# Landing x once and computing the forget sums with heads on partitions, in a decoder block on one core

## The chip, the cores and the metric

The kernel runs on one core of a Trainium2 chip. Its time is the device time of one execution in microseconds (us). Five engines matter. PE (TensorE) multiplies matrices: a weight load brings a stationary tile into the array, a matmul streams a moving tile through it, and the results go to PSUM, which has eight banks here (128 partitions by 512 fp32 words each). DVE (VectorE), ACT (ScalarE) and POOL (GpSimd) work elementwise, and SP (SyncE) issues DMAs. Each engine runs its own list of instructions in order, and waits on semaphores for what other engines or DMA queues have done.

## The reference: what is computed

One decoder layer on x, 256 tokens by 1024 channels, in fp32. With h = rms_norm(x), one projection gives q, k, v of two attention branches of 8 heads of 64, one forget logit per token and head, and two sets of gate logits. The first branch (moba) is, with 256 tokens and blocks of 256, plain causal softmax attention with a partial rotary embedding. The second one is what this change touches:

```python
log_f = jax.nn.log_sigmoid(f_logit + b_forget)      # (B, S, 8), then heads first
c = jnp.cumsum(log_f, axis=-1)                       # running sum over the tokens
s = einsum('bhcd,bhsd->bhcs', q, k) * HEAD_DIM**-0.5
s = s + c[t] - c[s]                                  # then causal mask and softmax
```

The two branch outputs go through their own output projections, are weighted with sigmoid gates, added, projected and added to x. A gated feed-forward layer with a causal convolution of width 3 follows.

## The kernel before

**Precision.** Each fp32 weight tile and each activation is split in a high part in fp32r and a low part (`whi`, `wlo`, `xh`, `xl`); a product is three matmuls (hi·hi, lo·hi, hi·lo). ACT writes `whi` (L123, a copy), DVE writes `wlo` (L124, raw minus `whi`) for every unit of weights. That is most of both engines' work.

**Loads.** Weights come by SP in the order of a list of units. A raw tile of 128x2048 (three buffers, tag `raw`) holds two units; a unit's split goes into one of six `whi`/`wlo` buffers, five units ahead of its use. The first eight units are the "heads": one DMA (two for heads 0 and 1) brings into one raw buffer, side by side, 256 tokens of the transposed x for 128 channels, the norm gain, and 1024 weight columns of q and k (L105). `split_x` makes `xh` and `xl` from x times gain (L155 to L158), `square_x` squares x on ACT (L162) and POOL adds the squares up (L164, L166). After the heads come the small tables (L192), and then the other weights.

**Stages.** `project_qk` (L233) multiplies the eight heads, `norm1` turns the sums of squares into `rs`, the norm factor of each token with tokens on partitions (L204). `project(m, ...)` (L243) then makes v, and q, k, v of the second branch; between them stand the small steps: `finish_qk` (norms and rotary), `turn_qk` (L291, transposes), the forget steps and the score matmuls of branch 0 (L393) with their softmax on DVE and ACT (L405 to L413; the profile's operation there is a fused add-and-minimum with an accumulator). `turn(0)` transposes the 48 blocks of probabilities into six banks (L423), ACT evicts them, and the gate matmuls (L457 to L459) begin.

**The forget steps.** `forget_a` loads nothing itself: the transposed x, `xT`, has come by two separate DMAs of 512 KB (L495), and eight small matmuls (L309) give the logits of the heads in four row groups of a bank. Two more matmuls (L312) spread `rs` over all partitions with tokens along the row; DVE copies it out as `rsB` (L315), which scales the gate logits later (L466). `forget_b` adds the row groups with two matmuls (L322), which puts tokens on partitions: everything up to the log sigmoid `lf` is 128 partitions by 2x8. `forget_c` makes the cumulative sum `cc` with three matmuls against a triangle and ones (L348 to L350). `forget_d` turns `cc` over (L356), DVE copies it out (L358), and two DMAs on ACT's queue write it to DRAM and read it back onto all partitions (L360, L362). `forget_bias` then makes the bias of the second branch's scores (L369, L371).

**What sets the order.** PE's order is that of the program (`manual_schedule`). The other engines' lists are made by a scheduler that places instructions by priority; what stands in a `with soon():` block comes 45 steps earlier in priority. PSUM tiles rotate through the eight banks, so a bank is written again only when the last reader of its earlier tile is done.

The lines that the change and the steps of the prediction touch:

Of the kernel before, what the change touches and what calls it, by code (L numbers as in the profile page):

```python
# [43 lines left out]
def decoder_block(ctx, tc, a, out):  # L44
# [52 lines left out]
    def load(upto):  # L97
        while state["next"] <= min(upto, len(units) - 1):
            c, h = units[state["next"]]
            if c[0] == "head":  # L100
                k = c[1]
                raw = T([P, 2048], "raw", RB)
                cuts = (0, HX + W4, HEADW) if k < 2 else (0, HEADW)
                for s0, s1 in zip(cuts, cuts[1:]):
                    loads[c] = nc.sync.dma_start(raw[:, s0:s1], a["head"][k][:, s0:s1])  # L105
                x, g, raw = raw[:, 0:S], raw[:, S:S + 1], raw[:, HX:HEADW]
# [32 lines left out]

    sm = T([P, C_END], "sm")  # L140
    g1 = T([P, KT], "g1")

# [47 lines left out]
    def tables():  # L190
        for t, n in ((sm, "smalls"), (cst, "consts"), (wfr, "wf"), (g1, "g1")):
            after(nc.sync.dma_start(t, a[n]), loads["head", KT - 1])  # L192
        nc.vector.tensor_scalar_mul(gq, sm[:, C_QG:C_QG + 4:2], -HD ** -0.5)
        nc.vector.tensor_tensor(wfg[:, :, 0:NH], wfr, g1[:, :, None].to_broadcast([P, KT, NH]), op=ALU.mult)
# [103 lines left out]
    gates = T([P, KT, 2, S], "gates")  # L298
# [6 lines left out]
    def forget_a():  # L305
# [4 lines left out]
        rp = fp[:, S:]  # L310
        for t in range(NT):
            nc.tensor.matmul(rp[:, t * P:(t + 1) * P], rs[:, t:t + 1].to_broadcast([P, P]), ident, start=True, stop=True)  # L312
        fs = gates[:, 0, 0]
        nc.vector.tensor_copy(fs, fp[:, :S])
        nc.vector.tensor_copy(rsB, rp)  # L315
        fg["fs"] = fs

    def forget_b():
        fs = fg["fs"]
        ft = bank()  # L320
        for t in range(NT):
            nc.tensor.matmul(ft[:, t * NH:(t + 1) * NH], fs[:, t * P:(t + 1) * P], sel, start=True, stop=True)  # L322
        z = T([P, NT, NH], "z")
        for t in range(NT):
            nc.vector.scalar_tensor_tensor(z[:, t], ft[:, t * NH:(t + 1) * NH], rs[:, t:t + 1], col(C_BF, NH), op0=ALU.mult, op1=ALU.add)

        az = T([P, NT, NH], "az")
        nc.scalar.activation(az, z, AF.Abs)
        e = T([P, NT, NH], "ez")
        nc.scalar.activation(e, az, AF.Exp, scale=-1.0)  # L330
        u = T([P, NT, NH], "uz")
        nc.vector.tensor_scalar_add(u, e, 1.0)
        l = T([P, NT, NH], "lz")
        nc.scalar.activation(l, u, AF.Ln)
        d = T([P, NT, NH], "dz")
        nc.vector.scalar_tensor_tensor(d, u, -1.0, e, op0=ALU.add, op1=ALU.subtract)
        r = T([P, NT, NH], "rz")
# [3 lines left out]
        lf = T([P, NT, NH], "lf")  # L341
        nc.vector.scalar_tensor_tensor(lf, z, 0.0, l, op0=ALU.min, op1=ALU.subtract)
        fg["lf"] = lf

    def forget_c():
        lf = fg["lf"]
        cp = bank()
        nc.tensor.matmul(cp[:, 0:8], tri, lf[:, 0], start=True, stop=True)  # L348
        nc.tensor.matmul(cp[:, 8:16], ones, lf[:, 0], start=True, stop=False)
        nc.tensor.matmul(cp[:, 8:16], tri, lf[:, 1], start=False, stop=True)  # L350
        nc.vector.tensor_copy(cc, cp[:, 0:16].rearrange("p (t h) -> p t h", t=NT))

    def forget_d():
        ctp = bank()
        for t in range(NT):
            nc.tensor.transpose(ctp[:8, t * P:(t + 1) * P], cc[:, t], ident)  # L356
        cT = gates[:NH, 1, 0]
        nc.vector.tensor_copy(cT, ctp[:8, :S])  # L358
        cd = dr.tile([NH, S], F32, name="cd")
        nc.scalar.dma_start(cd, cT)  # L360
        cB = gates[:, 4:].rearrange("p a b t -> p (a b) t")
        nc.scalar.dma_start(cB, bass.AP(tensor=cd.tensor, offset=cd.offset, ap=[[0, P], [S, NH], [1, S]]))  # L362
        fg["cB"] = cB
# [116 lines left out]
    pq, pk, pv = banks(), banks(), banks()  # L480
    for k in range(KT):
# [3 lines left out]
    with soon():  # L485
        norm1()
        qn, kn = finish_qk(0, ((0, pq), (1, pk)))
# [6 lines left out]
    for j in range(2):  # L494
# [237 lines left out]
```

## Time and profile before

| what | value |
|---|---|
| median of three runs | 365.48 us (365.46 to 365.97) |
| the profiled execution | 365.81 us, its span 364.0 us |
| granted clock | 1.0 |
| PE busy | 359.7 us, 99% of the span |
| DVE busy | 271.4 us, 75% |
| ACT busy | 215.3 us, 59% |
| POOL busy | 17.5 us, 5% |
| HBM read | 67.69 MB, 189 GB/s over the span |

The span runs from the first to the last instruction of the profiled execution; its time is 1.8 us longer, which lies around it. A row of the timeline gives start, length, engine, line, operation, output and input tiles, shapes and a count, and in brackets the idle time of the engine before it with what ended it. The lengths of pipelined instructions overlap, so the time an instruction takes on its engine is read from one start to the next.

### The profile page before, as it was taken

What the parts mean: (1) busy time and instruction counts of PE and PEld (TensorE: products, weight loads), DVE (VectorE), ACT (ScalarE), POOL (GpSimd) and SP (SyncE); (2) the same over time, 40 slices, a digit from 0 to 9 for tenths busy, and PEclk for the clock granted to TensorE, in tenths of its full rate; (3) what the DMA queues carried; (4) which work ended last, traced back from release to release, by engine and by line L of the source; (5) the groups of instructions that cost most, each with busy time, mean ns of one, the idle gap of its engine ahead of it and who ended that gap; (6) DMA issues with size and microseconds to landing.
All of it is one profiled execution on the core that took longest, in us unless ns stands there. A gap on an engine that the chain in (4) does not pass through costs nothing.

```text
span 364.0 us, 7218 instructions
## 1 busy us (share of the span) xinstructions
PE 359.7 (99%) x2975; PEld 340.2 (93%) x2975; DVE 271.4 (75%) x471; ACT 215.3 (59%) x358; POOL 17.5 (5%) x21
## 2 busy tenths in 40 slices
PE   9999999999999999999999999999999999999996
PEld 5888878888999999999999999999999999999995
DVE  4858998981999656984979867777686777768653
ACT  5748686776559885544867645545555545546420
POOL 0540000000000000000430000000000000000000
PEclk9999999999999999999999999999999999999999
DMA  8798875436081663645654554645645654644003
GB/s 281 236 337 314 325 298 196 158 117 233 2 330 25 232 225 115 220 159 204 230 177 170 206 186 188 232 147 202 230 157 194 230 174 176 230 170 180 1 2 115
DMA packets 11425, 69.21 MB, mean 190 GB/s; under 512 B 1528, under 2 KB 1920, under 8 KB 3968
## 3 DMA queue, kind: packets, MB, share of 16 engines
q1 hardware_dynamic: 11232, 67.69, 51.6%
q10 hardware_dynamic: 160, 1.06, 0.8%
q8 instruction: 23, 0.38, 0.4%
q14 instruction: 10, 0.08, 0.1%
HBM read 67.69 MB, written 1.06 MB: 189 GB/s over the span
## 4 chain that ended last, share of the span: by engine, by line
PE 99%; DVE 0%; issue 0%
PE bank L457 15%; PE bank L459 15%; PE bank L458 15%; PE bank L243 12%; PE bank L233 6%; PE bank L647 6%; PE bank L645 5%; PE bank L646 5%; PE bank L549 2%; PE bank L575 2%; PE bank L550 2%; PE bank L576 2%; PE bank L551 2%; PE bank L577 2%; PE bank L393 2%; PE bank L439 2%
## 5 line engine op out<-in xcount | busy, mean ns | idle before, releaser
L124 DVE TENSOR_TENSOR wlo<-raw,whi 128x1024 fp32r<-128x1024 f32 (+1 forms) x124 | 149.3, 1211 | 48.3 <-ACT whi L123 46.7
L123 ACT ACTIVATE whi<-raw 128x1024 fp32r<-128x1024 f32 (+1 forms) x124 | 128.5, 1044 | 85.5 <-PE bank L458 45.8
L457 PE MATMUL bank<-oh,whi 128*128 128x256 f32 x352 | 97.1, 276 | 0.0
L459 PE MATMUL bank<-oh,wlo 128*128 128x256 f32 x352 | 97.0, 275 | 0.0
L458 PE MATMUL bank<-ol,whi 128*128 128x256 f32 x352 | 97.0, 275 | 0.0
L457 PEld LDWEIGHTS bank<-oh,whi 128*128 128x128 f32 x352 | 66.1, 188 | 0.0
L458 PEld LDWEIGHTS bank<-ol,whi 128*128 128x128 f32 x352 | 66.1, 188 | 0.0
L459 PEld LDWEIGHTS bank<-oh,wlo 128*128 128x128 f32 x352 | 66.1, 188 | 0.0
L457 PE MATMUL bank<-xh,whi 128*128 128x256 f32 x128 | 35.8, 279 | 0.0
L459 PE MATMUL bank<-xh,wlo 128*128 128x256 f32 x128 | 35.3, 276 | 0.0
L458 PE MATMUL bank<-xl,whi 128*128 128x256 f32 x128 | 35.3, 276 | 0.0
L457 PEld LDWEIGHTS bank<-xh,whi 128*128 128x128 f32 x128 | 24.0, 188 | 0.5 <-DVE gates L466 0.3
L458 PEld LDWEIGHTS bank<-xl,whi 128*128 128x128 f32 x128 | 24.1, 188 | 0.0
L459 PEld LDWEIGHTS bank<-xh,wlo 128*128 128x128 f32 x128 | 24.0, 188 | 0.0
L243 PE MATMUL bank<-whi,xh 128*128 128x512 f32 x64 | 20.1, 395 | 0.0
L612 DVE TENSOR_TENSOR sq<-bank,rs 128x512 f32<-128x512 f32 x22 | 15.1, 692 | 6.6 <-PE bank L459 6.5
L243 PE MATMUL bank<-whi,xl 128*128 128x512 f32 x64 | 19.7, 389 | 0.0
L243 PE MATMUL bank<-wlo,xh 128*128 128x512 f32 x64 | 19.7, 389 | 0.0
L549 PE MATMUL bank<-oh,whi 128*128 128x256 f32 x64 | 17.8, 277 | 0.0
L550 PE MATMUL bank<-ol,whi 128*128 128x256 f32 x64 | 17.6, 276 | 0.0
L551 PE MATMUL bank<-oh,wlo 128*128 128x256 f32 x64 | 17.6, 276 | 0.0
L645 PE MATMUL bank<-kT,whi 128*128 128x256 f32 x64 | 17.6, 276 | 0.0
(161 smaller groups left out, 730.1 us busy)
## 6 DMA issues: line engine op xcount, KB each, us to landing
raw<-in_wu SPq DMA_DIRECT2D x22, 1024.0 KB, 4.8
raw<-in_wd SPq DMA_DIRECT2D x11, 1024.0 KB, 4.8
raw<-in_qkv SPq DMA_DIRECT2D x8, 1024.0 KB, 6.8
raw<-in_wg SPq DMA_DIRECT2D x8, 1024.0 KB, 4.8
raw<-in_wb SPq DMA_DIRECT2D x4, 1024.0 KB, 4.8
raw<-in_wo SPq DMA_DIRECT2D x4, 1024.0 KB, 4.9
raw<-in_head SPq DMA_DIRECT2D x6, 644.0 KB, 4.9
xT<-in_xT SPq DMA_DIRECT2D x2, 512.0 KB, 6.8
```

The costliest lines, as they stand in the source:

```text
L123: i = nc.scalar.activation(hi[:, s], raw[:, s], AF.Copy)
L124: d = nc.vector.tensor_tensor(lo[:, s], raw[:, s], hi[:, s].bitcast(F32), op=ALU.subtract)
L233: nc.tensor.matmul(pt[t], lhs[:, k, t * P:(t + 1) * P], rhs, start=(k == 0 and i == 0), stop=(k == KT - 1 and i == 2))
L243: nc.tensor.matmul(pt[t], lhs[:, k, t * P:(t + 1) * P], rhs, start=(k == 0 and i == 0), stop=(k == KT - 1 and i == 2))
L457: nc.tensor.matmul(o, wh[:, w], mh[:, k], start=(k == 0 and i == 0), stop=False)
L458: nc.tensor.matmul(o, wh[:, w], ml[:, k], start=False, stop=False)
L459: nc.tensor.matmul(o, wl[:, w], mh[:, k], start=False, stop=(k == KT - 1 and i == 1))
L549: nc.tensor.matmul(o, wh[:, w], oh[:, 4 * br + k], start=(k == 0), stop=False)
L550: nc.tensor.matmul(o, wh[:, w], ol[:, 4 * br + k], start=False, stop=False)
L551: nc.tensor.matmul(o, wl[:, w], oh[:, 4 * br + k], start=False, stop=(k == 3))
L645: nc.tensor.matmul(o, wh[:, w], ah, start=(p == 0 and h == 0 and c == 0), stop=False)
L647: nc.tensor.matmul(o, wl[:, w], ah, start=False, stop=(last and h == 1 and d == ds[-1]))
```

## The change

x lands once. Heads 0 and 1 land in the space of `gates`, which is not used until later, and POOL copies their x into `xT`. For heads 2 to 7 x lands directly in `xT` by a DMA of its own, and the weights take half a raw buffer. The gain `g1` comes first, by a DMA on ACT's queue. The two DMAs of `xT` are gone.

`rsB` comes by DRAM: after `norm1` POOL's queue carries two DMAs of 128 words into `rd` and one that reads it back onto all partitions. L312 and L315 are gone.

The forget sums stand with heads on partitions: one matmul (`sel` stationary, the 256 tokens moving) gives 8 partitions by 256, the log sigmoid is computed in that shape in rows of `gates`, and a scan on DVE along the tokens replaces the triangle matmuls. `cT` goes to DRAM and back by two DMAs on POOL's queue, as soon as the scan is done. `cc` (tokens on partitions) comes from two small transposes of `cT`, where `forget_d` was. The bias of the logits lies as a column on 8 partitions.

```diff
--- before.py
+++ after.py
@@ -99,11 +99,19 @@
             c, h = units[state["next"]]
             if c[0] == "head":
                 k = c[1]
-                raw = T([P, 2048], "raw", RB)
-                cuts = (0, HX + W4, HEADW) if k < 2 else (0, HEADW)
-                for s0, s1 in zip(cuts, cuts[1:]):
-                    loads[c] = nc.sync.dma_start(raw[:, s0:s1], a["head"][k][:, s0:s1])
-                x, g, raw = raw[:, 0:S], raw[:, S:S + 1], raw[:, HX:HEADW]
+                if k < 2:
+                    raw = gates[:, 4 * k:4 * k + 4].rearrange("p a b t -> p (a b t)")
+                    for s0, s1 in ((0, HX + W4), (HX + W4, HEADW)):
+                        loads[c] = nc.sync.dma_start(raw[:, s0:s1], a["head"][k][:, s0:s1])
+                    x, g, raw = raw[:, 0:S], raw[:, S:S + 1], raw[:, HX:HEADW]
+                    nc.gpsimd.tensor_copy(xT[:, k], x)
+                else:
+                    if k % 2 == 0:
+                        state["raw"] = T([P, 2048], "raw", RB)
+                    raw = state["raw"][:, k % 2 * 1024:(k % 2 + 1) * 1024]
+                    x, g = xT[:, k], g1[:, k:k + 1]
+                    nc.sync.dma_start(x, a["head"][k][:, 0:S])
+                    loads[c] = nc.sync.dma_start(raw, a["head"][k][:, HX:HEADW])
                 xlo = split_x(k, x, g)
                 at, n = 44, 2 if k < 2 else 1
             else:
@@ -137,8 +145,10 @@
         return split.pop((c, h))
 
 
+    gates = T([P, KT, 2, S], "gates")
     sm = T([P, C_END], "sm")
     g1 = T([P, KT], "g1")
+    nc.scalar.dma_start(g1, a["g1"])
 
     def col(c, n=1):
         return sm[:, c:c + n]
@@ -188,7 +198,7 @@
     gq = T([P, 2], "gq")
 
     def tables():
-        for t, n in ((sm, "smalls"), (cst, "consts"), (wfr, "wf"), (g1, "g1")):
+        for t, n in ((sm, "smalls"), (cst, "consts"), (wfr, "wf")):
             after(nc.sync.dma_start(t, a[n]), loads["head", KT - 1])
         nc.vector.tensor_scalar_mul(gq, sm[:, C_QG:C_QG + 4:2], -HD ** -0.5)
         nc.vector.tensor_tensor(wfg[:, :, 0:NH], wfr, g1[:, :, None].to_broadcast([P, KT, NH]), op=ALU.mult)
@@ -295,7 +305,6 @@
             nc.scalar.activation(dst[:, h], src, AF.Copy, scale=g)
 
 
-    gates = T([P, KT, 2, S], "gates")
     rsB = T([P, S], "rsB")
     bias = T([P, NH, 384], "bias")
     cc = T([P, NT, NH], "cc")
@@ -307,60 +316,42 @@
         for k in range(KT):
             r = slice(32 * (k % 4), 32 * (k % 4 + 1))
             nc.tensor.matmul(fp[r, :S], wfg[:, k], xT[:, k], start=(k < 4), stop=(k >= 4))
-        rp = fp[:, S:]
-        for t in range(NT):
-            nc.tensor.matmul(rp[:, t * P:(t + 1) * P], rs[:, t:t + 1].to_broadcast([P, P]), ident, start=True, stop=True)
         fs = gates[:, 0, 0]
         nc.vector.tensor_copy(fs, fp[:, :S])
-        nc.vector.tensor_copy(rsB, rp)
         fg["fs"] = fs
 
+    def row(i):
+        return gates[:NH, i // 2, i % 2]
+
     def forget_b():
-        fs = fg["fs"]
-        ft = bank()
-        for t in range(NT):
-            nc.tensor.matmul(ft[:, t * NH:(t + 1) * NH], fs[:, t * P:(t + 1) * P], sel, start=True, stop=True)
-        z = T([P, NT, NH], "z")
-        for t in range(NT):
-            nc.vector.scalar_tensor_tensor(z[:, t], ft[:, t * NH:(t + 1) * NH], rs[:, t:t + 1], col(C_BF, NH), op0=ALU.mult, op1=ALU.add)
-
-        az = T([P, NT, NH], "az")
-        nc.scalar.activation(az, z, AF.Abs)
-        e = T([P, NT, NH], "ez")
+        ft = bank()[:NH, 0:S]
+        nc.tensor.matmul(ft, sel, fg["fs"], start=True, stop=True)
+        bf = col(C_BF)[:NH]
+        z, az, e, u, l, d, r = (row(i) for i in range(1, 8))
+        nc.vector.tensor_tensor(z, ft, rsB[:NH], op=ALU.mult)
+        nc.scalar.activation(az, z, AF.Abs, bias=bf)
         nc.scalar.activation(e, az, AF.Exp, scale=-1.0)
-        u = T([P, NT, NH], "uz")
         nc.vector.tensor_scalar_add(u, e, 1.0)
-        l = T([P, NT, NH], "lz")
         nc.scalar.activation(l, u, AF.Ln)
-        d = T([P, NT, NH], "dz")
         nc.vector.scalar_tensor_tensor(d, u, -1.0, e, op0=ALU.add, op1=ALU.subtract)
-        r = T([P, NT, NH], "rz")
         nc.vector.reciprocal(r, u)
         nc.vector.tensor_tensor(d, d, r, op=ALU.mult)
         nc.vector.tensor_tensor(l, l, d, op=ALU.subtract)
-        lf = T([P, NT, NH], "lf")
-        nc.vector.scalar_tensor_tensor(lf, z, 0.0, l, op0=ALU.min, op1=ALU.subtract)
-        fg["lf"] = lf
+        nc.vector.tensor_scalar(z, z, bf, 0.0, op0=ALU.add, op1=ALU.min)
+        nc.vector.tensor_tensor(z, z, l, op=ALU.subtract)
+        cT = T([NH, S], "cT")
+        nc.vector.tensor_tensor_scan(cT, nc.const_aps.tensor(1.0, (NH, S), F32), z, 0.0, ALU.mult, ALU.add)
+        cd = dr.tile([NH, S], F32, name="cd")
+        nc.gpsimd.dma_start(cd, cT)
+        cB = gates[:, 4:].rearrange("p a b t -> p (a b) t")
+        nc.gpsimd.dma_start(cB, bass.AP(tensor=cd.tensor, offset=cd.offset, ap=[[0, P], [S, NH], [1, S]]))
+        fg.update(cT=cT, cB=cB)
 
     def forget_c():
-        lf = fg["lf"]
-        cp = bank()
-        nc.tensor.matmul(cp[:, 0:8], tri, lf[:, 0], start=True, stop=True)
-        nc.tensor.matmul(cp[:, 8:16], ones, lf[:, 0], start=True, stop=False)
-        nc.tensor.matmul(cp[:, 8:16], tri, lf[:, 1], start=False, stop=True)
-        nc.vector.tensor_copy(cc, cp[:, 0:16].rearrange("p (t h) -> p t h", t=NT))
-
-    def forget_d():
-        ctp = bank()
+        cp = bank()[:, 0:16]
         for t in range(NT):
-            nc.tensor.transpose(ctp[:8, t * P:(t + 1) * P], cc[:, t], ident)
-        cT = gates[:NH, 1, 0]
-        nc.vector.tensor_copy(cT, ctp[:8, :S])
-        cd = dr.tile([NH, S], F32, name="cd")
-        nc.scalar.dma_start(cd, cT)
-        cB = gates[:, 4:].rearrange("p a b t -> p (a b) t")
-        nc.scalar.dma_start(cB, bass.AP(tensor=cd.tensor, offset=cd.offset, ap=[[0, P], [S, NH], [1, S]]))
-        fg["cB"] = cB
+            nc.tensor.transpose(cp[:, t * NH:(t + 1) * NH], fg["cT"][:, t * P:(t + 1) * P], ident[:NH, :NH])
+        nc.vector.tensor_copy(cc, cp.rearrange("p (t h) -> p t h", t=NT))
 
     def forget_bias():
 
@@ -478,12 +469,16 @@
         return [bank() for _ in range(NT)]
 
     pq, pk, pv = banks(), banks(), banks()
+    rd = dr.tile([NT, P], F32, name="rd")
     for k in range(KT):
         project_qk(k, (pq, pk))
         if k == 2:
             tables()
     with soon():
         norm1()
+        for t in range(NT):
+            nc.gpsimd.dma_start(rd[t], rs[:, t])
+        nc.gpsimd.dma_start(rsB, bass.AP(tensor=rd.tensor, offset=rd.offset, ap=[[0, P], [1, S]]))
         qn, kn = finish_qk(0, ((0, pq), (1, pk)))
     project(2, pv, 0)
     project(2, pv, 1)
@@ -491,8 +486,6 @@
     pq, pk, pv = banks(), banks(), banks()
     project(3, pq, 0)
     project(3, pq, 1)
-    for j in range(2):
-        after(nc.sync.dma_start(xT[:, 4 * j:4 * j + 4], a["xT"][:, 4 * j:4 * j + 4]), loads["qkv", 1, 1])
     turn_qk(qn, 0, 0)
     with soon():
         forget_a()
@@ -506,13 +499,12 @@
     project(4, pk, 1)
     with soon():
         kn, = finish_qk(1, ((1, pk),))
-        forget_c()
         scores(0, (2, 3))
     project(5, pv, 0)
     project(5, pv, 1)
     finish_v(pv, 1)
     with soon():
-        forget_d()
+        forget_c()
         forget_bias()
     turn(0)
     gate(0)
...
@@ -696,7 +688,8 @@
-    sm[:, C_BF:C_BF + 8] = i["b_forget"][0][None]
+    sm[:, C_BF:C_BF + 8] = 0.0
+    sm[0:8, C_BF] = i["b_forget"][0]
```

The host's layout no longer makes the separate copy of x.

Three places show how the lists of the engines move. Names are those of the program; line numbers of the change are its own. First PE, at the end of the fifth of six transposed banks and the begin of the sixth in `turn(0)` (`bank_909` before, `bank_899` now; a number counts tiles, and `DVE_49` is the semaphore that DVE's instructions count up). Before:

```order
L423 MATMUL bank_907<-cst_168,s_787 128x64
L423 MATMUL bank_908<-cst_168,s_787 128x64 [waits DVE_49,Activation_49]
L423 MATMUL bank_909<-cst_168,s_787 128x64 [waits DVE_49]
L423 MATMUL bank_908<-cst_168,s_787 128x64
L423 MATMUL bank_909<-cst_168,s_787 128x64
L423 MATMUL bank_908<-cst_168,s_804 128x64
```

Now:

```order
L414 MATMUL bank_897<-cst_172,s_780 128x64
L414 MATMUL bank_898<-cst_172,s_780 128x64 [waits DVE_49]
L414 MATMUL bank_899<-cst_172,s_780 128x64 [waits DVE_49]
L414 MATMUL bank_898<-cst_172,s_780 128x64
L414 MATMUL bank_899<-cst_172,s_780 128x64
L414 MATMUL bank_898<-cst_172,s_797 128x64
```

The sixth bank waits for DVE in both: it is the bank that the transposes of `forget_d` (before) and of `forget_c` (now) filled just ahead of `turn(0)`, so the 34th of the 48 transposes waits for DVE's copy out of it, L358 before and L354 now.

Second DVE, from the first step of the log sigmoid on, with the softmax of the first pair between (`ISA` is the fused add-and-minimum, and the row `nm` behind it reads its accumulator). Before:

```order
L325 SCALAR_TENSOR_TENSOR z<-bank,rs,sm 128x8 x2
L124 TENSOR_TENSOR wlo<-raw,whi 128x1024
L332 TENSOR_SCALAR uz<-ez 128x16
L405 ISA s,nm<-bank,cst 128x128
L405 ISA nm 128x1
L336 SCALAR_TENSOR_TENSOR dz<-uz,ez 128x16
L338 RECIPROCAL rz<-uz 128x16
L405 ISA s,nm<-bank,cst 128x256
```

Now:

```order
L331 TENSOR_TENSOR gates<-bank,rsB 8x256
L132 TENSOR_TENSOR wlo<-raw,whi 128x1024
L334 TENSOR_SCALAR gates<-gates 8x256
L340 TENSOR_SCALAR gates<-gates,sm 8x256
L336 SCALAR_TENSOR_TENSOR gates<-gates 8x256
L337 RECIPROCAL gates<-gates 8x256
L396 ISA s,nm<-bank,cst 128x128
L396 ISA nm 128x1
L338 TENSOR_TENSOR gates<-gates 8x256
L396 ISA s,nm<-bank,cst 128x256
```

The steps stand in nearly the same places; each row has 256 words per partition where it had 16, and the reciprocal now stands ahead of the first softmax piece.

Third DVE, at the end of the four softmaxes of branch 0. Before:

```order
L410 RECIPROCAL r<-l 128x4
L124 TENSOR_TENSOR wlo<-raw,whi 128x1024
L413 TENSOR_SCALAR s<-s,r 128x128
L413 TENSOR_SCALAR s<-s,r 128x256
L413 TENSOR_SCALAR s<-s,r 128x128
L413 TENSOR_SCALAR s<-s,r 128x256
L124 TENSOR_TENSOR wlo<-raw,whi 128x1024 x2
L358 COPY gates<-bank 8x256
L124 TENSOR_TENSOR wlo<-raw,whi 128x1024
```

Now:

```order
L132 TENSOR_TENSOR wlo<-raw,whi 128x1024
L401 RECIPROCAL r<-l 128x4
L132 TENSOR_TENSOR wlo<-raw,whi 128x1024
L404 TENSOR_SCALAR s<-s,r 128x128
L404 TENSOR_SCALAR s<-s,r 128x256
L404 TENSOR_SCALAR s<-s,r 128x128
L404 TENSOR_SCALAR s<-s,r 128x256
L132 TENSOR_TENSOR wlo<-raw,whi 128x1024
L354 COPY cc<-bank 128x16
L132 TENSOR_TENSOR wlo<-raw,whi 128x1024
```

From the first of the log sigmoid's steps to the copy out of the bank DVE splits six units of weights before and five now.

More of the change, by code (lines that the diff above doesn't have):

```diff
@@ L672, in _layout @@
     c = np.ascontiguousarray
-    a = {"xT": c(k128(x.T))}
+    a = {}
     qkv = w[:, :6 * W4].reshape(2, 4, P, 6, W4)
```

## The prediction

> **What bounds the kernel now.** I read first the page's busy times and its chain of waits, then the waits of PE, then the timelines of PE and DVE around the steps that change. Page, parts 1 and 4, and the waits of PE's matmuls and weight loads (engine, tile, line, what ended the wait: us in total, times, longest):
>
> ```profile
> span 364.0 us, 7218 instructions
> PE 359.7 (99%) x2975; PEld 340.2 (93%) x2975; DVE 271.4 (75%) x471; ACT 215.3 (59%) x358; POOL 17.5 (5%) x21
> PE 99%; DVE 0%; issue 0%
> PEld bank L233 <- ACT whi L123: 0.6, 1, 0.6
> PEld bank L312 <- issue: 0.4, 1, 0.4
> PEld bank L457 <- DVE gates L466: 0.3, 1, 0.3
> PEld bank L233 <- DVE wlo L124: 0.3, 1, 0.3
> ```
>
> PE is the chain. Weight loads run ahead of matmuls, so the last rows are upper bounds of what PE lost. So a removed matmul is worth what PE's starts say, and waits of DVE, ACT and SP are worth nothing unless PE stands behind them. The changed kernel has two sides: PE has less to do, and DVE has more to do just before something that PE needs.
>
> **What PE loses in work.** Its timeline at the four places (start us, length, engine, line, count):
>
> ```profile
> 51.52 0.71 PE L312 MATMUL bank<-cst,rs 128*128 128x128 f32 x4
> 52.16 0.72 PE L291 MATMUL bank<-cst,qn 64*128 64x64 f32 x16
> 58.38 0.51 PE L322 MATMUL bank<-cst,gates 128*128 128x8 f32 x4
> 58.81 0.72 PE L393 MATMUL bank<-kT,qT 64*128 64x128 f32 x8
> 65.89 0.28 PE L348 MATMUL bank<-lf,cst 128*128 128x8 f32 x2
> 66.55 0.49 PE L393 MATMUL bank<-kT,qT 64*128 64x128 f32 x4
> 79.06 0.38 PE L356 MATMUL bank<-cst,cc 128*8 128x128 f32 x2
> 79.37 1.72 PE L423 MATMUL bank<-cst,s 64*128 64x64 f32 x48
> 81.02 0.39 PE L457 MATMUL bank<-xh,whi 128*128 128x256 f32 x1
> 188.47 0.59 PE L604 MATMUL bank<-sqs,cst 128*128 128x256 f32 x2
> 188.71 0.47 PE L457 MATMUL bank<-oh,whi 128*128 128x256 f32 x1
> ```
>
> From start to start: L312 takes 52.16 - 51.52 = 0.64. The weight load's 0.4 of issue there comes with the change of tile shape behind L309, which stays, so 0.53 to 0.64 goes. L348 to L350 take 66.55 - 65.89 = 0.66; a shape change stays there too, so 0.57 to 0.66 goes. L322 takes 0.43; the matmul in its place streams 256 words in fp32. The nearest row is L604's: two passes begin at 188.47, and the next matmul's start at 188.71 is within them (issues overlap), the lengths run to 0.59. I take 0.43, hence nothing saved, bounds 0 and 0.2. L356 takes 0.31 and is replaced by two transposes of 8 columns; L423's 48 transposes take (81.02 - 79.37) / 48 = 0.034 each, a switch of shape stays, so I take 0.1 saved, bounds 0 and 0.2. Sum 1.1 to 1.7, I take 1.3.
>
> **The early loads.** "No load waits for a buffer" is worth something if PE waits for such a load. Rows of PE, ACT, POOL and DVE in the head stage:
>
> ```profile
> 9.24 0.51 ACT L157 ACTIVATE xh<-raw 128x256 fp32r<-128x256 f32 x1 [0.45 <-DMA raw<-in_head]
> 8.37 0.61 PE L233 MATMUL bank<-whi,xh 128*128 128x512 f32 x2
> 11.09 0.61 PE L233 MATMUL bank<-whi,xh 128*128 128x512 f32 x2
> 12.01 0.74 PE L233 MATMUL bank<-wlo,xh 128*128 128x512 f32 x2
> 12.59 0.62 PE L233 MATMUL bank<-whi,xh 128*128 128x512 f32 x2
> 4.21 0.49 DVE L158 SCALAR_TENSOR_TENSOR xl<-raw,xh 128x256 fp32r<-128x256 f32 x1
> 5.52 1.05 PE L233 MATMUL bank<-whi,xl 128*128 128x512 f32 x2
> 11.88 0.96 DVE L158 SCALAR_TENSOR_TENSOR xl<-raw,xh 128x256 fp32r<-128x256 f32 x1
> 11.08 1.47 POOL L166 TENSOR_TENSOR xss<-xss,sq 128x256 f32<-128x256 f32 x1 [1.19 <-ACT sq L162]
> ```
>
> Head 2 lands at 9.24 and PE begins it at 11.09: the load leads PE by 1.9 us already. PE's only slip is from 12.01 to 12.59, 0.58 where the others take 0.45 (8.37 to 11.09 is six steps): 0.13 to be won at most. I take 0.
>
> Against it stand two copies of x on POOL, while DVE makes `xl` and `wlo` of heads 0 and 1. The `xl` row takes 0.49 alone and 0.96 beside POOL's 1.47. So POOL's copies can cost DVE about 0.5 each. At head 0 `xl` is done at 4.70 and PE streams from 5.52 on with it, 0.8 later. I take 0.1 of stall over both heads, bounds 0 and 0.6; it pays for what the first term may bring. [...]
>
> **The copy that now stands late.** The order of the lists shows that the sixth bank of `turn(0)` is the one that the small transposes filled, so the 34th of 48 transposes waits for DVE's copy out of it. Before, PE reached that transpose at 79.37 + 33 x 0.034 = 80.5, and DVE's copy was done at 79.88 (row below), 0.6 earlier; it had itself waited 0.68 for PE, so DVE was free at 79.47 - 0.68 = 78.79. Now PE comes 1.3 earlier, at 79.2. When DVE's copy L354 comes follows from the same rows:
>
> ```profile
> 58.92 0.36 DVE L325 SCALAR_TENSOR_TENSOR z<-bank,rs,sm 128x8 f32<-128x8 f32 x2 [0.93 <-PE bank L322]
> 59.21 1.23 DVE L124 TENSOR_TENSOR wlo<-raw,whi 128x1024 fp32r<-128x1024 f32 x1
> 60.63 0.17 DVE L336 SCALAR_TENSOR_TENSOR dz<-uz,ez 128x16 f32<-128x16 f32 x1
> 60.72 0.25 DVE L338 RECIPROCAL rz<-uz 128x16 f32<-128x16 f32 x1
> 60.88 0.37 DVE L405 CUSTOM_DVE_ANT_0 s<-bank,cst 128x256 f32<-128x256 f32 x1
> 62.81 0.18 DVE L410 RECIPROCAL r<-l 128x4 f32<-128x4 f32 x1
> 64.57 0.18 DVE L410 RECIPROCAL r<-l 128x4 f32<-128x4 f32 x1 [0.34 <-ACT s L408]
> 43.26 0.42 DVE L272 TENSOR_TENSOR p<-qn,rc 128x256 f32<-128x256 f32 x1
> 43.59 0.42 DVE L273 TENSOR_TENSOR p<-qn,rsn 128x256 f32<-128x256 f32 x1
> 79.47 0.41 DVE L358 COPY gates<-bank 8x256 f32<-8x256 f32 x1 [0.68 <-PE bank L356]
> ```
>
> Two readings first. DVE's time goes by words per partition, not by partitions: 8x256 took 0.41 (L358), 128x256 took 0.42 (L272). And starts lie about 0.085 closer than lengths (60.63 to 60.72 is 0.09 for a length of 0.17; 43.26 to 43.59 is 0.33 for 0.42). So a step of the log sigmoid that took 0.09 now takes 0.33, and turning the layout over saves no work on DVE but multiplies it.
>
> Added: the product for z, d, d·r, l-d and z-l at 0.33 each, 1.65; u and the minimum, with one tensor input, at most as much, 0.55 to 0.66. The reciprocal took 0.18 - 0.085 = 0.09 for 4 words and 0.16 for 16 (60.72 to 60.88), 5.8 ns a word, so 0.16 + 240 x 0.0058 = 1.55 for 256 (by the lengths, 0.25 + 240 x 0.006 = 1.7). Of the scan the trace has nothing; its bounds are a plain two-input row, 0.33, and the reciprocal's rate, 1.6; nearest is a two-input row, and since each word needs the one before it, I take 0.6. The sum is 4.4 to 4.5 (4.2 to 5.5). Gone: z 0.29, uz, dz, dz·r, lz, lf at 0.09 each, the reciprocal's 0.16, and the copy of `cc` 0.09, together 1.0. Also one split of weights fewer stands ahead of the copy (1.23 - 0.085 = 1.14), and with the list fuller the 0.34 that DVE idled at 64.57 goes, and perhaps as much again in small gaps.
>
> DVE needed 78.79 - 58.92 = 19.87 from z to the copy. Now 19.87 + 4.45 - 1.0 - 1.14 - 0.34 to 0.7 = 21.5 to 21.8. z starts earlier by what L312 saved, at 58.3 to 58.4. So the copy begins at 79.8 to 80.2 and lets PE go 0.2 later, at 80.0 to 80.4, where PE stood ready at 79.2: a stall of 0.8 to 1.2, I take 1.0. Behind it nothing is late next: the gate matmuls need weights that DVE split long before, and ACT's evictions of the other five banks run on.
>
> [...]
>
> **What else moves, at nothing.** `rsB` by DRAM is issued when `rs` is ready near 31 us, and z needs it at 58.3. `cB` comes earlier: in the rows that follow, DVE idled 8.73 for it.
>
> ```profile
> 30.85 0.16 DVE L204 SCALAR_TENSOR_TENSOR rs<-rsv 128x2 f32<-128x2 f32 x1
> 89.85 2.36 DVE L369 TENSOR_TENSOR bias<-gates,cc 128x1024 f32<-128x1024 f32 x2 [8.73 <-DMA gates<-cd]
> gates<-cd ACTq DMA_DIRECT2D x1, 1024.0 KB, 7.1
> ```
>
> That idle time was not PE's: PE's waits hold only 0.3 at L457 for `gates`, worth at most 0.1 to 0.3 when the bias no longer delays the eviction. SP issues 16 head transfers instead of 10 and two of 512 KB fewer; loads lead PE, so nothing. Uncovered, a late `rsB` would hold DVE at z, then its splits, then PE one for one.
>
> **The sum.** -1.3 of PE work, +1.0 of stall at the sixth bank, 0 at the start (+0.1 - 0.1): -0.3. The profiled execution's 365.81 (span 364.0) becomes 365.5; it lies 0.3 above the median of the runs, 365.48, which becomes **365.2**. A difference under 0.2% (0.73 us) can't be told from none here, so the forecast is no change that can be measured.
>
> **Rivals.**
> 1. *The stall does not come.* If the scheduler's list is met earlier than I add up (the scan and reciprocal near a plain row's 0.33: 1.2 + 0.3 less; further gaps filled), the copy comes before 79.2 or little after. For it: no row has a reciprocal or a scan of 256 words. Against it: the two reciprocal rows grow with the words. Then -1.3, with the 0.3 at the gates up to -1.6: 364.2 (363.9 to 364.7).
> 2. *DVE becomes the bound there and takes more than PE gave.* [...] With the scan at 1.6, no gap filled and z at 58.4, it begins at 58.4 + 19.87 + 5.5 - 1.0 - 1.14 = 81.6, the stall is 2.6 and the time 365.5 - 1.3 + 2.6 = 366.8. For it: a wide list with one late reader. Against it: it needs the worst of two bounds.
> 3. *`rsB` comes late.* POOL's queue holds four small transfers; before, `gates<-cd` took 7.1 on ACT's queue. Even three of these in a row, 21 us behind 31, end at 52, before 58.3. From 58.3 on the cost is one for one. [...] A z that starts 3 us late makes the copy and the sixth bank 3 us late: 368.2.
> 4. *The early loads bring what the change names.* Then the 0.13 at 12.01 and a part of the start's 0.6 go besides, at most 0.7: 364.6. Against it: the lead of 1.9 us.
>
> **How the numbers follow.** The forecast (stall 0.5 to 1.7, hence -0.8 to +0.4) has 0.55, 364.7 to 365.9. Rival 1 has 0.24, rival 4 0.04, rival 2 0.14, rival 3 0.03. Faster by over 0.2% is rivals 1 and 4 and a little of the forecast, 0.30; slower is rivals 2 and 3 in part, 0.15; the rest is no change, 0.55. The range takes rival 1's and rival 2's near halves: 364.1 to 366.3.
>
> **What would show it.** PE's timeline should have the rows of L312, L348 to L350 and L356 gone and `turn(0)` begin about 1.3 earlier, near 78.1 instead of 79.4. In the waits of PE a new row should stand, L414 for DVE's `cc`, of 0.8 to 1.2. DVE's reciprocal 8x256 should read 1.5 to 1.8, its plain 8x256 rows 0.42, the scan 0.4 to 0.8. The bias rows should have lost their 8.7 of idle. Wrong would be: no wait at L414 (rival 1), a copy past 81 (rival 2), z waiting for a DMA (rival 3), or a first head stage that ends more than 0.2 off 27.7.

## The result and the profile after

The changed kernel takes 368.29 us (median of 5 runs, 368.18 to 368.67) against 365.80 us (5 runs, 365.46 to 366.04) for the kernel before: a ratio of 1.0068, 95% interval 1.0049 to 1.0087. It is 2.5 us slower, where the prediction had 365.2 and no change that can be measured. The profiled execution took 368.20 us, with a span of 366.4.

The page of the changed kernel, parts 1 and 4:

```profile
span 366.4 us, 7206 instructions
PE 358.9 (98%) x2963; PEld 338.2 (92%) x2963; DVE 274.9 (75%) x470; ACT 215.1 (59%) x358; POOL 19.1 (5%) x28
PE 92%; DVE 6%; issue 0%; DVEq 0%
```

PE's work shrank by 0.8 us, from 359.7. But the chain of waits, 99% PE before, now holds 6% of DVE. The waits of PE and its weight loads say where (engine, tile, line, what ended the wait: us, times, longest):

```profile
PE bank L301 <- DVE qn L285: 1.5, 1, 1.5
PE bank L414 <- DVE cc L354: 1.2, 1, 1.2
PEld bank L253 <- DVE nm L396: 0.6, 2, 0.3
```

The second row is the wait that was forecast. The first and third were not. PE's timeline at the same markers as in the prediction (before: 52.16, 58.81, 66.55, 79.37 and 81.02):

```profile
52.27 0.71 PE L301 MATMUL bank<-cst,qn 64*128 64x64 f32 x16 [1.48 <-DVE qn L285]
59.09 1.60 PE L384 MATMUL bank<-kT,qT 64*128 64x128 f32 x16
66.29 2.11 PE L384 MATMUL bank<-kT,qT 64*128 64x128 f32 x16
68.33 0.97 PE L253 MATMUL bank<-whi,xh 128*128 128x512 f32 x2
79.88 1.28 PE L414 MATMUL bank<-cst,s 64*128 64x64 f32 x33
82.31 0.71 PE L414 MATMUL bank<-cst,s 64*128 64x64 f32 x15 [1.15 <-DVE cc L354]
82.95 0.39 PE L448 MATMUL bank<-xh,whi 128*128 128x256 f32 x1
```

| marker | before | after | after - before | z1 (below) - before |
|---|---|---|---|---|
| end of the heads' projection | 27.56 | 26.76 | -0.80 | -0.04 |
| second turn of the first branch | 52.16 | 52.27 | +0.11 | -0.68 |
| scores 0, 1 | 58.81 | 59.09 | +0.28 | -0.47 |
| scores 2, 3 | 66.55 | 66.29 | -0.26 | -1.06 |
| first transpose of turn(0) | 79.37 | 79.88 | +0.51 | -1.06 |
| gate matmuls | 81.02 | 82.95 | +1.93 | -0.55 |
| last matmul | 360.18 | 362.11 | +1.93 | -0.57 |

So the profiled loss of 2.4 us has three main pieces. Between the first two markers PE saved 0.64 (L312) and still lost 0.91, so 1.55 of waiting. Between scores 2, 3 and `turn(0)` it lost 0.77, of which 0.53 had come by the next projection's start at 68.33 (68.06 before). In `turn(0)` it lost 1.42. Another 0.45 lies behind the last matmul (3.8 us to the span's end before, 4.3 after) and 0.17 ahead of scores 0, 1. Against these stand the 0.80 at the first marker and 0.54 between the two pairs of scores, where L348 to L350 are gone.

The cause of the first piece is in the stretch before it. The same stretches of both kernels (stretch; its length; busy us of PE, PEld, DVE, ACT, POOL with instructions; granted clock, DMA share, GB/s), before and then after:

```profile
33.00:36.00 3.00, 3.00 (x15) 2.47 (x14) 3.00 (x5) 3.00 (x5) 0.00 (x0) 1.00 0.87 332
36.00:39.00 3.00, 3.00 (x15) 2.50 (x14) 3.00 (x5) 2.81 (x6) 0.00 (x0) 1.00 0.78 288
39.00:42.00 3.00, 3.00 (x15) 2.50 (x14) 2.90 (x7) 1.15 (x2) 0.00 (x0) 1.00 0.83 284
```

```profile
33.00:36.00 3.00, 3.00 (x15) 2.49 (x14) 3.00 (x6) 3.00 (x6) 0.00 (x0) 1.00 1.13 41
36.00:39.00 3.00, 3.00 (x15) 2.47 (x14) 2.86 (x6) 1.12 (x4) 0.00 (x0) 1.00 0.42 38
39.00:42.00 3.00, 3.00 (x15) 2.48 (x14) 0.00 (x0) 0.34 (x1) 0.55 (x1) 1.00 0.63 216
```

There is a hole in the DMA traffic: 38 to 41 GB/s where there were 288 to 332, while the DMA engines' share of busy time is up to 1.13 (the times of packets are added up, so a share above 1 means that they overlap). Packets are under way for long and move little: in the packed trace the longest packet of a load takes 6.4 us, where none took over 1.9 before. The new loads themselves are not the cause. They do leave the queues empty from 30 to 33 us (0 GB/s after, and in x1, x5 and z1 below, which lack these writes), but in x1 the next two stretches carry traffic:

```profile
33.00:36.00 3.00, 3.00 (x15) 2.49 (x14) 3.00 (x5) 3.00 (x5) 0.00 (x0) 1.00 0.71 240
36.00:39.00 3.00, 3.00 (x15) 2.47 (x14) 2.93 (x7) 1.13 (x4) 0.00 (x0) 1.00 0.84 279
```

What stands around the hole, in the timelines of POOL, ACT and DVE after:

```profile
28.82 1.26 POOL L480 DMA_DIRECT2D rd<-rs  x2 [7.85 <-DVE rs L214]
39.07 0.55 POOL L481 DMA_DIRECT2D rsB<-rd  x1 [8.99 <-DMA rd<-rs]
43.08 2.01 ACT L131 ACTIVATE whi<-raw 128x1024 fp32r<-128x1024 f32 x2 [3.73 <-DMA raw<-in_qkv]
44.17 1.23 DVE L132 TENSOR_TENSOR wlo<-raw,whi 128x1024 fp32r<-128x1024 f32 x1 [5.25 <-ACT whi L131]
45.31 1.28 DVE L275 TENSOR_TENSOR qn<-bank,qf 128x512 f32<-128x512 f32 x2
51.93 0.29 DVE L285 TENSOR_TENSOR qn<-p,p 128x128 f32<-128x128 f32 x1
```

The two writes of `rs` to DRAM, 1 KB in all, take 9 us to land. A weight tile issued at 32.5 lands at 43.08, 10.6 us later (in x1 these tiles take at most 5.0). In DVE's list the split of that tile stands ahead of the norm step `qn`, so DVE idles 5.25 us, `qn` begins at 45.31 (41.45 before), and the last rotary step ends at 52.2, after PE wants it. `rsB` itself is not late for anyone: issued at 39.07, it landed 6.8 us later, 15 us before z.

### The profile page after: what moved, and what is told of

Read it like the earlier page. It is cut to its first block, busy times and chain, and to the rows that moved or that the text cites. A ratio compares the mean times of both kernels' runs of the same rounds, so it can differ in the third digit from the quotient of the medians.

```text
span 366.4 us, 7206 instructions
## 1 busy us (share of the span) xinstructions
PE 358.9 (98%) x2963; PEld 338.2 (92%) x2963; DVE 274.9 (75%) x470; ACT 215.1 (59%) x358; POOL 19.1 (5%) x28
## 3 DMA queue, kind: packets, MB, share of 16 engines
HBM read 66.75 MB, written 1.06 MB: 185 GB/s over the span
## 4 chain that ended last, share of the span: by engine, by line
PE 92%; DVE 6%; issue 0%; DVEq 0%
PE bank L448 15%; PE bank L449 15%; PE bank L450 15%; PE bank L253 8%; PE bank L243 6%; PE bank L638 5%; PE bank L639 5%; PE bank L637 5%; PE bank L541 2%; PE bank L567 2%; PE bank L542 2%; PE bank L543 2%; PE bank L569 2%; PE bank L568 2%; DVE wlo L132 2%; PE bank L430 2%
## 5 line engine op out<-in xcount | busy, mean ns | idle before, releaser
L132 DVE TENSOR_TENSOR wlo<-raw,whi 128x1024 fp32r<-128x1024 f32 x120 | 147.0, 1227 | 57.0 <-ACT whi L131 56.8
L131 ACT ACTIVATE whi<-raw 128x1024 fp32r<-128x1024 f32 x120 | 126.0, 1057 | 83.5 <-PE bank L449 49.9
L448 PE MATMUL bank<-xh,whi 128*128 128x256 f32 x128 | 35.7, 279 | 0.0
L567 PE MATMUL bank<-xh,whi 128*128 128x256 f32 x64 | 17.6, 275 | 0.0
```

The lines of the kernel that those rows point to most:

```text
L131: i = nc.scalar.activation(hi[:, s], raw[:, s], AF.Copy)
L132: d = nc.vector.tensor_tensor(lo[:, s], raw[:, s], hi[:, s].bitcast(F32), op=ALU.subtract)
L448: nc.tensor.matmul(o, wh[:, w], mh[:, k], start=(k == 0 and i == 0), stop=False)
L567: nc.tensor.matmul(o, wh[:, w], mh[:, k], start=(k == 0 and i == 0), stop=False)
```

## The experiments

**Theory W**: the 256 writes of 4 bytes hold up the DMA engines and with them other loads. **Rival O**: the order on DVE alone, a split ahead of the rotary steps. **Rival D**: the wide forget steps on DVE.

**x1: one part undone.** In the changed kernel, `rsB` by matmuls again:

```diff
-            nc.gpsimd.dma_start(rd[t], rs[:, t])
-        nc.gpsimd.dma_start(rsB, ...)
+            nc.tensor.matmul(rp[:, t * P:(t + 1) * P], rs[:, t:t + 1].to_broadcast([P, P]), ident, ...)
+        nc.vector.tensor_copy(rsB, rp)
```

> The change with one part undone: rsB comes from the two matmuls and the copy again, no trip of rs by DRAM. Theory W (the 256 writes of 4 bytes from rs to DRAM hold up all DMA engines, so that the weights issued at 32 to 38 us land 5 us late, and DVE with them): the DMA traffic has no hole between 31 and 40 us, PE's wait of 1.5 us at the second turn of the first branch is gone, z starts near 58.5 instead of 60.9, the wait for cc shrinks to about 0.5, time 365.3 to 366.0. Rival O (a split of weights now stands ahead of the norm and rotary steps on DVE, whatever the DMAs do): the wait of 1.5 stays, time 367.5 to 368.5. Rival D (the wide forget steps on DVE alone make the loss): the wait of 1.5 goes or stays, time 367 or more.

Measured: 365.9 us, ratio to before 0.9996 (0.9983 to 1.001). In its waits of PE the row of L301 is gone, and of the copy this is left:

```profile
PE bank L418 <- DVE cc L358: 0.2, 1, 0.2
```

All of the loss went with this one part, though the split still stands ahead of `qn` on DVE (which idles 1.40 us for it) and the forget steps are as wide. O and D fall.

**x2: the two writes on ACT's queue**, the read back as in the change:

```diff
-            nc.gpsimd.dma_start(rd[t], rs[:, t])
+            nc.scalar.dma_start(rd[t], rs[:, t])
```

> The change with the two writes of rs to DRAM issued on ACT's queue, everything else (the read back on POOL's queue too) as in the change. Theory W in its form that the small writes themselves are slow: the hole in the DMA traffic stays, 6 to 9 us wide, and the time stays at 367.5 to 368.7. In its other form, that POOL's software queue is slow: the hole goes, the landing of rd takes 2 to 3 us instead of 9, time 365.3 to 366.2. Rival O: hole or not, 367.5 to 368.5.

Measured: 368.55 us, 1.0079 (1.005 to 1.0107). The traffic has the same hole:

```profile
36.00:39.00 3.00, 3.00 (x15) 2.47 (x14) 3.00 (x4) 2.16 (x6) 0.71 (x1) 1.00 0.51 60
```

So it isn't that POOL's queue issues the writes.

**x3: the disputed cost by itself**, in the kernel before; nothing reads `rd`:

```diff
         norm1()
+        rd = dr.tile([NT, P], F32, name="rd")
+        for t in range(NT):
+            nc.gpsimd.dma_start(rd[t], rs[:, t])
```

> The kernel before, and only the two writes of rs to DRAM on POOL's queue added; nobody reads what they write. Theory W: a hole of 6 to 9 us in the DMA traffic after 31 us, loads of that stretch land 5 us late, time plus 0.5 to 2.5 (the order on DVE is the one before, where the split of weights stands behind the rotary steps, so less than in the change). Rivals O and D: no hole that matters, within 0.3 of before.

Measured: 370.92 us, 1.0126 (1.0108 to 1.0144). Writing 1 KB that nobody reads costs some 5 us, more than the range I gave. Its stretches, and its one new wait of PE of any length:

```profile
36.00:39.00 3.00, 3.00 (x15) 2.49 (x14) 3.00 (x5) 2.85 (x6) 0.00 (x0) 1.00 1.53 46
39.00:42.00 3.00, 3.00 (x15) 2.49 (x14) 2.90 (x7) 1.14 (x2) 0.00 (x0) 1.00 0.95 35
42.00:45.00 3.00, 3.00 (x15) 2.48 (x14) 3.00 (x8) 0.00 (x0) 0.00 (x0) 1.00 0.61 30
```

```profile
PE bank L309 <- DMA xT<-in_xT: 4.7, 1, 4.7
```

Here the victim is the separate load of `xT`, which the change does away with. The wait is not the whole price. In the profiled execution (372.2 us, the longest of the four) PE was 5.05 us late at the matmuls of L312 just behind it, and 1.3 us more by 60.20: the granted clock is 0.55 in 56:58 and 0.59 in 58:60, and L312 takes 1.15 us where it took 0.64. Behind the waits of 1.5 us and less in the changed kernel the granted clock stays at 1.00. So such a hole costs some 5 us with the loads of before, and 2.4 (against x1) to 3.1 (against z1) with those of the change.

**x4 and x5: the other two parts alone**, in or beside the kernel before with `rsB` from matmuls. x4 has the new forget sums and the old loads, x5 the new loads and the old forget sums.

> The kernel before with the forget sums of the change alone (heads on partitions, scan, two small transposes); loads as before and rsB from the two matmuls. Theory W with the prediction's sum: PE work minus 0.7, a wait of 0.4 to 1.0 for the copy of cc at the sixth bank, so within 0.5 of before (365.3 to 366.0). Rival D: plus 1 to 2.5.

> The change's loads alone (x lands once, POOL's two copies, g1 first); rsB from the matmuls and the forget sums as before. By the prediction's working 365.3 to 365.8 against 365.6 for the kernel before: the loads led PE already, 0.13 to win. If the start of the projection gains what the change's trace shows (its first stage ended 0.8 us earlier), 364.6 to 365.0. If the split of weights ahead of the rotary steps costs by itself (rival O), 366 or more.

Measured: x4 366.14 us, 1.0024 (0.9999 to 1.0048); x5 365.49 us, 0.9992 (0.9984 to 1.0001). Neither can be told from no change. Rival D falls again, and the new loads bring nothing that is measured.

**x6: `rsB` from matmuls, and the copy of `cc` earlier:**

```diff
     project(5, pv, 0)
+    with soon():
+        forget_c()
     project(5, pv, 1)
     finish_v(pv, 1)
     with soon():
-        forget_c()
         forget_bias()
```

> rsB from the matmuls, and the two small transposes with their copy of cc one half of a projection earlier, so that the copy stands ahead of the last softmax pieces on DVE. Against the run with rsB from matmuls alone (365.9), whose wait for cc was 0.2 to 0.4: minus 0.2 to 0.5, 365.3 to 365.7, and no row of a wait of L418 for cc. If the late copy only passes its wait on to the next late thing on DVE: 365.8 to 366.2.

Measured: 365.51 us, 0.9994 (0.9985 to 1.0003); the wait of L418 for `cc` is gone. By the ratios it stands where x1 stands (0.9996), so what the earlier copy is worth by itself is lost in the noise.

**y1 to y8: what makes the writes slow.** All are the kernel before with unread writes as in x3, changed in one way, with one profiled execution each. The core of the edits:

```diff
 y1  one of the two writes:    for t in range(1)
 y2  pieces of 512 bytes:      nc.gpsimd.dma_start(rd[t], rsw)               # rd [2, 128, 128], rs in rsw[:, 0:2]
 y4  words 512 bytes apart:    nc.gpsimd.dma_start(rd[t][:, 0:1], rs[:, t:t+1])   # rd [2, 128, 128]
 y5  words 64 bytes apart:     the same with rd [2, 128, 16]
 y6  words 32 bytes apart:     the same with rd [2, 128, 8]
 y7  16 words per write:       nc.gpsimd.dma_start(rd[t, 0:16], rs[0:16, t])
 y8  128 pieces of 8 bytes:    nc.gpsimd.dma_start(rd, rs)                   # rd [128, 2]
```

> The kernel before and two writes to DRAM on POOL's queue as in the run with the unread writes, but each of the 256 pieces is 512 bytes instead of 4 (rs stands in the first two words of a row of 128; the rest is zero; nobody reads them). If the smallness of a piece is what is slow: no hole, landing in 3 to 5 us, 365.3 to 366.5. If the number of pieces is: hole as wide, 369 to 371.

> The kernel before and the two unread writes of 128 words of 4 bytes, with the words 512 bytes apart in DRAM instead of side by side. If pieces that share a line of DRAM wait for one another: no hole, landing in 2 to 4 us, 365.3 to 366.5. If any write of 4 bytes is slow: hole as wide, landing in 9 to 12 us, 369 to 371.

> The kernel before and the unread writes of 256 words, 64 bytes apart in DRAM. 512 bytes apart cost nothing (365.6, landing 4.7 us), side by side 5 us. If the unit within which writes hold one another up is 64 bytes or less: no hole, 365.3 to 366.5. If it is larger: a hole, in full 370, or shorter with fewer words to a unit.

> The kernel before and one of the two unread writes: 128 words of 4 bytes side by side. If the words wait for one another in turn, the hole and the landing take half: landing 5 to 7 us instead of 11.6, time 365.6 to 368. If the hole has a length of its own, landing 10 us or more and 369 to 371.

> The kernel before and the unread writes of 256 words, 32 bytes apart in DRAM. If writes hold one another up within 64 bytes: a hole, shorter than with the words side by side, landing 5.5 to 9 us. If within 32 bytes or less: no hole, landing 4.5 to 5 us, 365.2 to 366.5.

> The kernel before and two unread writes of 16 words each, side by side, 64 bytes in all for each. If the words of one 64-byte stretch wait in turn at about 0.5 us each (16 words, 8 to 9 us): the hole is as long as with 128 words, landing 9 to 12 us, 368 to 372. If the length goes with all the words: landing 2.5 to 4 us, 365.2 to 366.5.

> The kernel before and one unread write of 128 pieces of 8 bytes side by side (the same 1 KB in all as the two writes of words). If the pieces of one 64-byte stretch wait in turn: 8 pieces to a stretch instead of 16, landing and hole about half, 5 to 8 us. If the length is fixed or goes with the bytes: 10 to 12 us.

| run | pieces written | landing, us | GB/s in 33:36, 36:39, 39:42 | longest packet of a load, us | time, us |
|---|---|---|---|---|---|
| x3 | 256 of 4 bytes, side by side | 11.6 | 331, 46, 35 | 9.2 | 370.92 |
| y1 | 128 of 4 bytes, side by side | 10.7 | 407, 79, 44 | 7.7 | 371.76 |
| y8 | 128 of 8 bytes, side by side | 7.3 | 242, 27, 281 | 4.3 | 365.62 |
| y7 | 2 times 16 of 4 bytes, side by side | 5.6 | 231, 251, 385 | 2.2 | 365.13 |
| y6 | 256 of 4 bytes, 32 bytes apart | 5.3 | 185, 352, 410 | 1.5 | 365.20 |
| y5 | 256 of 4 bytes, 64 bytes apart | 4.8 | 179, 336, 423 | 1.8 | 365.23 |
| y4 | 256 of 4 bytes, 512 bytes apart | 4.7 | 268, 292, 380 | 1.4 | 365.60 |
| y2 | 256 of 512 bytes, side by side | 4.5 | 415, 290, 262 | 1.4 | 366.73 |

(Each time is of one execution, x3's is a median. y1 and y2 also lost 0.7 to 0.9 us to a late `whi` before the writes began, so their times are not read. The writes of y4 to y7 were issued at 29 to 31 us and have landed by 36.5, so the lower rates in 33:36 are theirs; but a dip of a microsecond or two stands at the seam of two loads in the kernel before as well, 213 and 143 GB/s in 35:36 and 36:37. The longest packet, from the packed traces, does not depend on where a stretch is cut; before, it is 1.9.) The plainest pair is x3 and y4: same 256 words, same queue, same shapes, only the place in DRAM differs. y4's stretch beside x3's first one above:

```profile
36.00:39.00 3.00, 3.00 (x15) 2.49 (x14) 3.00 (x5) 2.55 (x5) 0.00 (x0) 1.00 0.79 292
```

Neither the size of a piece nor their number makes the hole by itself: 256 words apart do no harm (y4 to y6), and 256 pieces of 512 bytes side by side do none (y2). The holes stood behind 128 or 256 pieces of 4 or 8 bytes side by side in DRAM: 27 to 79 GB/s in their 36:39 (x3, y1, y8). y8's is 3 to 4 us long, and its victims had enough lead. The time isn't a simple count: half the words (y1) hardly shortened it, 16 words per write (y7) took 0.9 longer than words apart and not the 8 to 9 us that waiting in turn within 64 bytes at a fixed price would need. Words apart are also spread over more than the 1 KB of x3 (8 KB in y6), and no run separates the two. What exactly waits for what stays open.

y4, y5 and y6 wrote pieces as small as x3's and landed in 4.7 to 5.3 us against 11.6: where the words lie matters too. And the same 256 words of 4 bytes into one row of SBUF landed in 2.0 us (z1).

**z1 and z2: the change without the hole.** z1 gathers `rs` in one row of SBUF first; z2 moves the copy of `cc` as in x6 besides.

```diff
+        rr = T([1, NT, P], "rr")
         for t in range(NT):
-            nc.gpsimd.dma_start(rd[t], rs[:, t])
+            nc.gpsimd.dma_start(rr[:, t], rs[:, t])
+        nc.gpsimd.dma_start(rd, rr)
         nc.gpsimd.dma_start(rsB, bass.AP(tensor=rd.tensor, offset=rd.offset, ap=[[0, P], [1, S]]))
```

> The change with one more hop for rsB: the 256 words of rs are first gathered into one row in SBUF (two DMAs of 128 pieces of 4 bytes on POOL's queue), the row goes to DRAM in 16 pieces of 64 bytes, and from there onto all partitions as in the change. Theory W in its sharper form (4-byte pieces side by side in DRAM hold one another up, and the other loads of the same DMA engines with them): no hole, PE's wait of 1.5 gone, what is left is the prediction's sum: PE minus 1.3, the wait for cc 0.4 to 1.0, so 364.8 to 365.6. If 4-byte pieces side by side are as slow in SBUF: the hole stays, 367.5 to 368.7.

> The same with the two small transposes and the copy of cc one half of a projection earlier. Theory: the wait for cc goes too, PE keeps its 1.3 less small waits: 364.2 to 365.0, below the kernel before. If the hole stays: 367 to 368.5.

Measured: z1 365.17 us, 0.9979 (0.996 to 0.9997); z2 364.94 us, 0.9981 (0.9972 to 0.9989); the kernel before had 365.58 beside them, so z2 is 0.6 us faster in the medians. z1 is the case that the prediction had in mind, a trip that holds up nothing else, and its median is the forecast 365.2. That they agree to the tenth is in part luck: terms that were off cancel (below). Its timeline on POOL, DVE and PE:

```profile
29.57 1.26 POOL L481 DMA_DIRECT2D rr<-rs  x2 [8.52 <-DVE rs L214]
32.80 0.51 POOL L482 DMA_DIRECT2D rd<-rr  x1 [1.96 <-DMA rr<-rs]
34.66 0.58 POOL L483 DMA_DIRECT2D rsB<-rd  x1 [1.35 <-DMA rd<-rr]
58.44 0.41 DVE L331 TENSOR_TENSOR gates<-bank,rsB 8x256 f32<-8x256 f32 x1 [0.53 <-PE bank L328]
79.62 0.15 DVE L354 COPY cc<-bank 128x16 f32<-128x16 f32 x1
78.31 1.28 PE L414 MATMUL bank<-cst,s 64*128 64x64 f32 x33
79.84 0.71 PE L414 MATMUL bank<-cst,s 64*128 64x64 f32 x15 [0.25 <-DVE cc L354]
80.47 0.38 PE L448 MATMUL bank<-xh,whi 128*128 128x256 f32 x1
```

Three hops instead of two, and `rsB` is on its way at 34.66, not at 39.07. In z2 the 48 transposes run through without a wait:

```profile
77.79 1.71 PE L414 MATMUL bank<-cst,s 64*128 64x64 f32 x48
```

## Why the prediction was wrong

**The step that failed** is the first sentence under "What else moves, at nothing": "`rsB` by DRAM is issued when `rs` is ready near 31 us, and z needs it at 58.3." It priced the trip by when its own result is needed. What it costs is what it does to other transfers on the same DMA engines: about 6 us of almost no traffic in the changed kernel (8 to 66 GB/s in each microsecond from 34 to 40), about 9 in x3. x3 shows the writes alone costing 5 us, x1 shows the loss gone without them, z1 shows 365.17 with the trip made in another way. The third rival named the right transfer and the wrong victim: `rsB` was in time, the weights were not. It had 0.03. No run shows a z that waits 3 us for `rsB`; in the change z came 2.49 us later than in z1, behind the late weights.

**The early loads** ("I take 0"): held. x5 is 0.9992 (0.9984 to 1.0001). POOL's copies did cost DVE something, but less than was feared, at another row, and nothing to PE:

```profile
3.75 0.57 DVE L165 TENSOR_SCALAR xh<-gates 128x256 fp32r<-128x256 f32 x1 [2.88 <-DMA gates<-in_head]
3.77 0.40 POOL L107 COPY xT<-gates 128x256 f32<-128x256 f32 x1 [2.61 <-DMA gates<-in_head]
4.35 0.48 DVE L168 SCALAR_TENSOR_TENSOR xl<-gates,xh 128x256 fp32r<-128x256 f32 x1
```

A POOL copy takes 0.40, not the 1.47 of the two-input row I took for it, and is over before `xl` begins. Beside it `xh` takes 0.57, in all seven kernels with these copies, against 0.35 in the ten without. `xl` is done at 4.83, and PE streams it from 5.20 on. `xl` takes 0.48 and did not meet the copy, so what a copy would cost it, 0.5 in the prediction's estimate, was not shown.

**PE's work** (1.3): about 1.02 in z1 (1.06 less the 0.04 of the first marker). L312 gave 0.64 and L348 to L350 0.59, as taken. The matmul that replaced L322 was taken at no change; up to the scores it lost 0.22 (from -0.69 at the projection ahead of it to -0.47), 0.12 of it ahead of the matmul's start and 0.10 behind. L356's 0.1 came (-0.97 to -1.06).

**The late copy** (stall 1.0): the mechanism held, the size was half. In z1 PE lost 0.51 in `turn(0)`. DVE went from z to the copy in 79.62 - 58.44 = 21.18, where I had 21.5 to 21.8, and z1's PE came 0.2 later than I had it. The second rival's 81.6 was a start of this copy as well; the change's, at 82.10, is past it and past the sign's 81, but for a late z, not for longer steps on DVE. The changed kernel's own rows give the same 82.10 - 60.93 = 21.17, and the price of each new form:

```profile
60.93 0.41 DVE L331 TENSOR_TENSOR gates<-bank,rsB 8x256 f32<-8x256 f32 x1
62.60 0.34 DVE L340 TENSOR_SCALAR gates<-gates,sm 8x256 f32<-8x256 f32 x1
63.20 1.73 DVE L337 RECIPROCAL gates<-gates 8x256 f32<-8x256 f32 x1
66.92 0.67 DVE L343 TENSOR_TENSOR_SCAN cT<-const-float32-1.0,gates 8x256 f32<-8x256 f32 x1
82.10 0.15 DVE L354 COPY cc<-bank 128x16 f32<-128x16 f32 x1
83.32 2.34 DVE L360 TENSOR_TENSOR bias<-gates,cc 128x1024 f32<-128x1024 f32 x2
```

The reciprocal's 1.73 was worked out as 1.55 to 1.7, from rows of 4 and 16 words; the scan's 0.67 (0.60 to the next start) was taken as 0.6. From start to start that is 0.60 where a plain two-input row takes 0.34, by the lengths 0.67 against 0.41. In the change the stall was 1.42 instead of z1's 0.51, because the hole had made z late: 60.93 against 58.44, 2.49 later, where PE came to `turn(0)` only 1.57 later. The difference, 0.92, is the 0.91 of added stall. The 0.53 at the scores (PE's weight loads behind `nm`) is taken for the same lateness: z1 does not have it.

**The bias** lost its 8.73 us of idle time on DVE (83.32, no wait), and PE gained nothing from it, as taken.

With z1's terms the sum reads -1.06 + 0.51 = -0.55 at the gate matmuls, where the prediction had -0.3. Both sides were too large, by 0.24 to 0.28 and 0.5, and their errors have opposite signs. Behind the last matmul z1's profile then loses 0.4 that no term had (end of this text), so that its span is 363.9 against 364.0. What lies near the forecast is the total, not each term.

## What to carry to other kernels

Price a small DMA not only by when its own data is needed, but by what it does to the DMA engines that all loads share: look at the GB/s of the stretches around it, and at the landing times of large loads issued at the same time. Don't write words from many partitions side by side into DRAM (x3: 11.6 us to land, and 5 us of time); gather them in a row of SBUF first (z1, z2: 2.0 us to land there, 1.6 from there to DRAM), or, by single executions of y4 to y6, lay them 32 bytes or more apart. And read each engine's new order for what now stands ahead of a critical step: a split ahead of `qn` cost nothing while its data was in time, and turned a late load into 1.5 us of PE's time when it was not.

## What the runs showed of the hardware that I had not expected

Writes of 4 bytes, side by side in DRAM, 256 of them, held all DMA traffic at 30 to 46 GB/s for some 9 us (x3, 36 to 45) and stretched a packet of a load to 9.2 us. The same words 32 bytes apart landed in 5.3 us, and no packet of a load took over 1.5 us (y6).

Two long waits of PE cost more than their length: behind 4.7 us (x3) and 3.3 us (y1) the granted clock was 0.50 to 0.68 in the stretches from 56 to 60 us and 1.00 again from 60 on; over either whole execution it was 0.995. Behind the waits of 1.2 and 1.5 us in the changed kernel it stayed at 1.00, and over x2's whole execution, with waits of 0.8 to 1.7 us, it was 0.999.

The first pairs of matmuls ran at a pace that differed from one profiled execution to the next: from its start to the next pair's, the first took from 0.54 us (x6) to 1.02 (before). Before and after:

```profile
4.50 1.22 PE L233 MATMUL bank<-whi,xh 128*128 128x512 f32 x2
5.52 1.05 PE L233 MATMUL bank<-whi,xl 128*128 128x512 f32 x2
6.38 0.80 PE L233 MATMUL bank<-wlo,xh 128*128 128x512 f32 x2
```

```profile
4.46 0.90 PE L243 MATMUL bank<-whi,xh 128*128 128x512 f32 x2
5.20 0.62 PE L243 MATMUL bank<-whi,xl 128*128 128x512 f32 x2
5.66 0.61 PE L243 MATMUL bank<-wlo,xh 128*128 128x512 f32 x2
```

That is the 0.80 of the first marker, and it is no gain of the change: over all profiled executions the heads' projection ended at 26.8 to 27.6 with the loads of before (10 kernels) and at 26.7 to 27.5 with those of the change (7 kernels). A difference of 0.8 us in a single profile, at the start, says nothing here. So the prediction's last sign of being wrong, a first head stage that ends more than 0.2 off 27.7, could not be one.

Behind the last matmul the span went on for 3.8 to 3.9 us in the kernel before and its variants with unread writes, and for 4.1 to 4.3 in all kernels with the new loads or the new forget sums. That 0.2 to 0.5 is part of the loss in each of them, z2 too; its cause stays open.
